# SSM tables and outputs in DRAM laid out for one transfer each, in a hybrid decoder layer on one core

## The chip, the core and the metric

The kernel runs on one core of a Trainium2 chip. The metric is the device time of one execution in microseconds (us); where several runs were made, their median. A profiled execution has its own time, and a span from its first to its last instruction that is a little shorter.

The engines are named as in the profile: PE multiplies matrices (PEld loads its weights), DVE works on vectors, ACT evaluates functions and copies, POOL is the general engine, SP issues transfers. Each engine runs its own list of instructions in order. An instruction that issues a DMA stands in such a list too, and those behind it wait for it.

## What is computed

One layer of a hybrid decoder over 1024 positions and 2048 channels, in float32:

```
h = rms_norm(x, norm_w);  proj = h @ w_in
q, k, v, a_gate, u, z, g_a, g_s = split(proj)
y_a = (window_attention(q, k, v, sinks) * silu(a_gate)) @ w_attn_proj
y_ssm = gelu(s5_ssm(u.reshape(b, l, 64 groups, 16)))          # 64 complex states in each group
glu_a, glu_b = split(y_ssm @ w_glu + b_glu)
y_s = (glu_a * sigmoid(glu_b) * silu(z)) @ w_ssm_proj
x = x + (sigmoid(g_a) * y_a + sigmoid(g_s) * y_s) @ w_out
```

`s5_ssm` runs, for each of the 64 groups, the diagonal recurrence s[t] = a s[t-1] + B u[t] with complex a (from A, log_dt), and gives y = Re(C s) + D u.

## The kernel before

**Projections.** Everything large is a product of 128 x 128 weight tiles with 512 positions. A float32 product is made of three: the weight and the activation are each split in a high and a low part (`split`, L80 to L82: ACT writes the high part by a cast, DVE the low part by a subtraction), and PE adds high x high, high x low and low x high (L121, L122, L125). `load_w` loads 512 KB of weights (8 tiles) by one DMA on SP (L106) into `wraw`, and the two casts make `whi` and `wlo`; each of the three has two buffers. Eight tiles are 24 matmuls of 512 columns.

**The stages** follow one another in the program: `uproj` (the SSM's input u) and the z gate with the preparation of the SSM tables beside them; `kvq` and attention; then the sigmoids and gates of the remaining columns with the SSM itself beside them; then the four products after it (`glu`, `att_out`, `ssm_out`, `out1` to `out3`), which split 2 x 2 blocks into seven products (Strassen), so that sums and differences of operand blocks have to be made first (`combos`).

**What sets the order.** The side work is written as generators that the main loop advances at given rates (`spawn`, `pull`, `drive`). Each engine's list is then fixed at build time by a scheduler that simulates the execution. An estimate of a shorter wait moves an instruction forward in its engine's list, and the engine then asks for its inputs earlier.

**The SSM in four batches of 16 groups.** `ssm_prep` computes powers of a (`wr`, `wi`; `p1`, `p2`; `al`, `be`), stores them in DRAM (PWD, PTD), and computes the table of the convolution within eight positions (`ks`), stored as KD behind 128 zeros. `ssm` does for each batch, in two halves q of eight groups:

- it loads the powers 16 times per half, eight times for the real and eight for the imaginary part, each to 16 partitions (`pwr`, `pwi`, L687), and B (`bre`, `bim`, L690);
- POOL makes `bm` from them in six operations (L665 by way of `tt`), PE multiplies it with u (`px`, L703), ACT copies the result to X;
- DVE and ACT run the recurrence on X;
- it loads `tz`, the shifted table, from KD by eight transfers (L744), POOL makes `ct`, PE makes `py` (L752, L753), ACT applies GELU to `yt`, and 16 transfers of 32 KB on SP store it in YD (L760).

`bm` and `tz` share one buffer, and `pwr`, `pwi`, `bre`, `bim`, `yt` have one each.

**What reads YD.** `combos` (L816) loads four 128 x 512 blocks (`cb_b`) for each of four k, DVE and POOL make four sums, and POOL stores them; it has five `cb` buffers. `load_ops` (L788) then loads operands (`op`) and splits them (`q1h`, `q6h`, ...: `q` and the number of the product).

**Constants for attention** (`c_qw`, `c_sk`, `c_blk`, `c_sel` and others) are loaded on POOL's queue after the last instructions of `ssm_prep`.

Of the kernel before, what the change touches and what calls it, by code (L numbers as in the profile page):

```python
# [9 lines left out]
F32 = mybir.dt.float32  # L10
# [14 lines left out]
NG = 64  # L25
# [7 lines left out]
def _build(nc, tc, I, OUT, ctx):  # L33
# [8 lines left out]
    dp = ctx.enter_context(tc.tile_pool(name="d", bufs=1, space=DRAM))  # L42
# [10 lines left out]
    CBD = {n: dp.tile([4, k, 128, TH], F32, name="cb" + n) for n, k in (("y", 4), ("a", 4), ("s", 4), ("m", 8))}  # L53
    QD = [dp.tile([8, 128, TH], F32, name=f"qd{n}") for n in range(3)]
    UD = dp.tile([8, 8, 128, NCH], F32, name="ud")
    YD = dp.tile([2, NG * 16, 8, 64], F32, name="yd")
    PWD = dp.tile([2, 8, NG, 64], F32, name="pwd")
    PTD = dp.tile([4, 128, 12, NG], F32, name="ptd")
    KD = dp.tile([16, NG, 256], F32, name="kd")

# [68 lines left out]
    def win(n):  # L129
        return [I["w_in"][n, :, c * KC:(c + 1) * KC, :] for c in range(2)]  # L130
# [89 lines left out]
    w = {(0, 0): load_w(win(12)[0], 2)}  # L220
    for kt in range(KT):
        if kt == 2:
            w[1, 0] = load_w(win(13)[0], 2)
        elif kt == 6 or kt == 8:
            n = kt // 8
# [228 lines left out]
    def ssm_prep(bp, pp):  # L454
        def tl(shape, tag, bufs=1, dt=F32, name=None):
            return bp.tile(list(shape), dt, tag=tag, bufs=bufs, name=name or tag)

        def tt(o, a, b, op, eng=None):
            (eng or V).tensor_tensor(o, a, b, op=op)
# [138 lines left out]
        cib = ci[0:64, 64:128].unsqueeze(1).to_broadcast([64, 8, 64])  # L598
        cmul(wr, wi, pr[0:64, 0:8, 64:128], pi[0:64, 0:8, 64:128], crb, cib, u2)
        for n, w in ((0, wr), (1, wi)):  # L600
            nc.gpsimd.dma_start(PWD[n].rearrange("j g p -> g j p"), w)

        p1, p2 = tl((128, 9, NG), "p1"), tl((128, 9, NG), "p2")
        V.tensor_copy(p1[0:64], pr[0:64, :, 0:64])
# [14 lines left out]
        for n in (9, 10, 11):  # L619
            p = slice(n - 1, n)  # L620
# [21 lines left out]
        for bt in range(4):  # L642
            ks = tl((16, GB, 8, 16), "ks")
            for q in range(GB // 8):
                g0 = bt * GB + q * 8
                ct = ctable(bp, tt, V, p1, p2, g0, 8, g0, 2)
                for qq in range(2):
                    pk = pp.tile([128, 4, 128], F32, tag="pa", bufs=2, name="pk")
                    for g in range(4):
                        gg = qq * 4 + g  # L650
                        PE.matmul(pk[0:16, g, :], bb[:, g0 + gg, :],
                                  ct[:, gg, 0:8, :].rearrange("p k h -> p (k h)"), start=True, stop=True)
                    S.copy(ks[:, q * 8 + qq * 4:q * 8 + qq * 4 + 4, :, :].rearrange("p g k h -> p g (k h)"),
                           pk[0:16])
                yield
            tt(ks[:, :, 0, :], ks[:, :, 0, :], dd[:, bt * GB:(bt + 1) * GB, :], add)
            nc.gpsimd.dma_start(KD[:, bt * GB:(bt + 1) * GB, 128:256],
                                ks.rearrange("p g k h -> p g (k h)"))

    def ssm(bp, pp):  # L660
        def tl(shape, tag, bufs=1, dt=F32, name=None):
            return bp.tile(list(shape), dt, tag=tag, bufs=bufs, name=name or tag)
# [6 lines left out]
        for bt in range(4):  # L669
            gs = bt * GB  # L670
# [11 lines left out]
            for q in range(2):  # L682
                g0 = gs + q * 8
                w = [tl((128, 8, 64), n, 1) for n in ("pwr", "pwi", "bre", "bim")]
                for n in range(2):
                    for j in range(8):
                        nc.sync.dma_start(w[n][16 * j:16 * j + 16],  # L687
                                          PWD[n, 7 - j, g0:g0 + 8, :].unsqueeze(0).to_broadcast([16, 8, 64]))
                for n, nm in ((2, "sBrT"), (3, "sBiT")):
                    nc.sync.dma_start(w[n], I[nm][:, g0:g0 + 8, :])  # L690
                bm = tl((128, 8, 2, 64), "bm", 1)
                u = tl((128, 8, 64), "bmu", 1)
                tt(bm[:, :, 0, :], w[0], w[2], mul, G)
                tt(u, w[1], w[3], mul, G)
                tt(bm[:, :, 0, :], bm[:, :, 0, :], u, sub, G)
                tt(bm[:, :, 1, :], w[0], w[3], mul, G)
                tt(u, w[1], w[2], mul, G)
                tt(bm[:, :, 1, :], bm[:, :, 1, :], u, add, G)
                for qq in range(2):
                    px = pp.tile([128, 4, 128], F32, tag="pa", bufs=2, name="px")  # L700
                    for g in range(4):
                        gg = qq * 4 + g
                        PE.matmul(px[:, g, :], bm[:, gg, :, :].rearrange("p a b -> p (a b)"),  # L703
                                  uq[:, q * 8 + gg, :], start=True, stop=True)
                    S.copy(X[:, q * 8 + qq * 4:q * 8 + qq * 4 + 4, :, 1:9, :].rearrange("p g h k s -> p g h (k s)"),
                           px.rearrange("p g (h c) -> p g h c", h=2))
                yield
# [32 lines left out]

            for q in range(2):
                tz = tl((128, 8, 128), "bm", 1, name="tz")
                for j in range(8):
                    nc.sync.dma_start(tz[16 * j:16 * j + 16],  # L744
                                      KD[:, gs + q * 8:gs + q * 8 + 8, 128 - 16 * j:256 - 16 * j])
                ct = ctable(bp, tt, G, p1, p2, gs + q * 8, 8, q * 8, 1)
                yt = tl((128, 8, NCH), "yt", 1)
                for qq in range(2):
                    py = pp.tile([128, 4, 128], F32, tag="pb", bufs=2, name="py")
                    for g in range(4):  # L750
                        gg = q * 8 + qq * 4 + g
                        PE.matmul(py[:, g, :], tz[:, qq * 4 + g, :], uq[:, gg, :], start=True, stop=False)  # L752
                        PE.matmul(py[:, g, :].rearrange("p (h c) -> p h c", h=2),  # L753
                                  ct[:, qq * 4 + g, 1:9, :].rearrange("p k h -> p (k h)"),
                                  X[:, gg, :, 0:8, :].rearrange("p h k s -> p h (k s)"), start=False, stop=True)
                    S.activation(yt[:, qq * 4:qq * 4 + 4, :], py, AF.Gelu_apprx_tanh)
                g0 = gs + q * 8
                for i in range(8):
                    for s in range(2):
                        nc.sync.dma_start(YD[s, g0 * 16:(g0 + 8) * 16, i, :].rearrange("(g h) c -> h g c", h=16),  # L760
                                          yt[16 * i:16 * i + 16, :, 64 * s:64 * s + 64])
                yield


# [10 lines left out]
    def unit(q, nk):  # L775
        p, t = (gp, "g") if q in IN_G[nk] else (hp, "h")
        return tuple(p.tile([128, TH], F32R, tag=t + x, name=f"q{q}{x}") for x in "hl")

    def load_ops(ops, src, nk, order, ks=None):

        todo = [(q, k) for q in order for k in ks or range(nk)]
        got = []

        def more(n):
            while todo and len(got) < n:
                q, k = todo.pop(0)
                t = staging()
                nc.sync.dma_start(t, src(q, k))  # L788
                got.append((q, t))

        more(STG - 1)
        yield
        while got:
            for _ in range(min(2, len(got))):
                q, t = got.pop(0)
                a, b = unit(q, nk)
                split(t, a, b)
                ops.setdefault(q, []).append((a, b))
                more(STG - 1)
            yield  # L800
# [10 lines left out]
    def combos(B, dst, nk):  # L811
        ct = lambda n: cbp.tile([128, TH], F32, tag="cb", bufs=5, name="cb_" + n)
        for k in range(nk):
            b = [ct("b") for _ in range(4)]
            for n, t in enumerate(b):
                nc.sync.dma_start(t, B(n // 2, n % 2, k))  # L816
            b11, b12, b21, b22 = b
            d7 = ct("d7")
            V.tensor_tensor(d7, b12, b22, op=SUB)
            G.tensor_tensor(b12, b11, b12, op=SUB)  # L820
            G.tensor_tensor(b22, b12, b22, op=ADD)
            V.tensor_tensor(b21, b21, b22, op=SUB)
            for n, t in enumerate((b12, b22, d7, b21)):
                nc.gpsimd.dma_start(dst[n, k], t)
            yield
# [364 lines left out]
    cbp = ctx.enter_context(tc.tile_pool(name="cb", bufs=1))  # L1190
    gp = ctx.enter_context(tc.tile_pool(name="g", bufs=12))
    p3 = ctx.enter_context(tc.tile_pool(name="p3", bufs=5, space=PSUM))
    By = lambda i, h, k: YD[h, (4 * i + k) * 128:(4 * i + k + 1) * 128].rearrange("p i c -> p (i c)")
    Ba = lambda i, h, k: AGD[h][4 * i + k]
    Bs = lambda i, h, k: SD[h][4 * i + k]
    Bm = lambda i, h, k: MD[h][8 * i + k]
# [36 lines left out]
def _layout(inputs):  # L1233
    A = {k: np.asarray(v) for k, v in inputs.items()}
# [7 lines left out]
    uc = ar(1024).reshape(8, 8, 16).transpose(0, 2, 1).reshape(-1)  # L1242
# [3 lines left out]
    def tiles(w):  # L1246
        k, n = w.shape
        return cc(w.reshape(k // 128, 128, n // 128, 128).transpose(2, 1, 0, 3))

    o = {}  # L1250
    o["xT"] = cc(A["x"][0].T).reshape(KT, 128, T)
    o["w_in"] = tiles(A["w_in"][:, cols])
    o["w_attn"] = tiles(A["w_attn_proj"][hc])
    o["w_glu"] = tiles(A["w_glu"])
    o["w_ssm"] = tiles(A["w_ssm_proj"])
    o["w_out"] = tiles(A["w_out"])
    o["nw"] = cc(A["norm_w"].reshape(KT, 128).T)
# [6 lines left out]
    i = ar(128)  # L1264
# [42 lines left out]
```

## Time and profile before

| | |
|---|---|
| three runs | 2544.15, 2546.79, 2549.72 us (median 2546.79) |
| profiled execution | 2542.53 us; its span 2540.8 us |
| busy share of the span | PE 97%, PEld 79%, DVE 61%, ACT 38%, POOL 36% |
| mean granted clock of PE | 0.988 of full speed |
| transfers | 438.95 MB, mean 173 GB/s |
| preparation of the tables | to about 205 us |
| SSM beside the projections | about 862 to 1360 us |
| combos and operands from YD | about 1360 to 1430 us, and 1732 to 1742 us |

Times within the execution count from the start of the span. A busy PE says little by itself, because matmuls overlap and their ends are modelled; the number of matmuls in a stretch tells whether it ran at its pace. A name in a row such as `px<-uq,bm` is what is written and what it is made from; `x16` is the count; `[3.38 <-POOL bm L665]` is idle time just before and what ended it.

### The profile page before, as it was taken

The numbers are of one execution on the slowest core, as the hardware profiler recorded it, in microseconds if no ns is written. First come the engines' busy times: TensorE is split into PE (matmuls) and PEld (weight loads), VectorE is DVE, ScalarE is ACT, GpSimd is POOL, SyncE is SP. The second block draws the span as 40 slices with busy tenths as digits, with TensorE's granted clock in tenths as the row PEclk, the third lists the DMA queues.
The fourth block names the chain that finished last, engine by engine and source line by source line (L and its number), as shares of the span: only waits on it lengthen the run. The fifth ranks groups of instructions, "written<-read, shape, count | busy, mean of one in ns | idle before, by whom it ended". The sixth has DMA issues, their size and how long they took to land. (4 is left out here: it accounts for less than half of the span.)

```text
span 2540.8 us, 30817 instructions
## 1 busy us (share of the span) xinstructions
PE 2459.2 (97%) x11012; PEld 2007.1 (79%) x11012; DVE 1557.5 (61%) x2040; ACT 963.8 (38%) x1492; POOL 921.5 (36%) x715
## 2 busy tenths in 40 slices
PE   7999999999999999999999999999999999899998
PEld 5878878788878878888788788887878877678886
DVE  7995566894686455736573432236587687745543
ACT  5333454463666433434442222224352331333311
POOL 5101004341453434251412300014547466414576
PEclk9999999999999999999999999999999999999999
DMA  6544343323223456565757743336368676888675
GB/s 212 177 135 133 92 141 104 96 72 99 96 92 121 141 161 165 177 166 142 206 159 240 259 164 124 120 120 216 108 223 296 203 252 227 266 298 278 222 234 176
DMA packets 217306, 438.95 MB, mean 173 GB/s; under 512 B 63521, under 2 KB 75841, under 8 KB 217153
## 3 DMA queue, kind: packets, MB, share of 16 engines
q1 hardware_dynamic: 181376, 344.34, 44.4%
q0 software_dynamic: 19504, 63.28, 6.6%
q10 hardware_dynamic: 16272, 29.38, 3.0%
q8 instruction: 86, 1.41, 0.2%
q14 instruction: 68, 0.55, 0.1%
HBM read 341.93 MB, written 94.96 MB: 172 GB/s over the span
## 5 line engine op out<-in xcount | busy, mean ns | idle before, releaser
L121 PE MATMUL ps<-hh,whi 128*128 128x512 f32 x2144 | 845.3, 395 | 4.7 <-ACT whi L81 4.7
L122 PE MATMUL ps<-hl,whi 128*128 128x512 f32 x2144 | 842.1, 393 | 1.0 <-DVE hl L144 1.0
L82 DVE TENSOR_TENSOR wlo<-wraw,whi 128x1024 fp32r<-128x1024 f32 (+1 forms) x344 | 445.2, 1295 | 488.9 <-PE ps L125 247.7
L81 ACT CAST whi<-wraw 128x1024 fp32r<-128x1024 f32 (+1 forms) x344 | 349.8, 1018 | 637.2 <-PE ps L122 372.0
L125 PE MATMUL ps<-hh,wlo 128*128 128x512 f32 x2144 | 542.0, 391 | 1.7 <-DVE wlo L82 1.7
L121 PEld LDWEIGHTS ps<-hh,whi 128*128 128x128 f32 x2144 | 405.1, 189 | 93.8 <-ACT whi L81 6.4
L122 PEld LDWEIGHTS ps<-hl,whi 128*128 128x128 f32 x2144 | 405.3, 189 | 86.7 <-DVE hl L144 2.1
L125 PEld LDWEIGHTS ps<-hh,wlo 128*128 128x128 f32 x2144 | 401.5, 188 | 86.9 <-DVE wlo L82 2.1
L81 ACT CAST whi<-ws 128x1024 fp32r<-128x1024 f32 x80 | 84.2, 1054 | 292.5 <-POOL ws L855 80.4
L82 DVE TENSOR_TENSOR wlo<-ws,whi 128x1024 fp32r<-128x1024 f32 x80 | 116.4, 1456 | 115.7 <-ACT whi L81 74.4
L855 POOL TENSOR_TENSOR ws<-wraw 128x512 f32<-128x512 f32 (+1 forms) x72 | 135.0, 1875 | 132.9 <-DVE wlo L82 95.8
L421 POOL TENSOR_TENSOR pa<-ph,c_mct 128x512 fp32r<-128x512 f32 x32 | 43.7, 1364 | 253.3 <-ACT ph L81 253.2
L178 POOL DMA_DIRECT2D gsd<-sg x32 | 17.8, 556 | 226.7 <-ACT sg L177 214.8
L177 ACT ACTIVATE sg<-sg 128x512 f32<-128x512 f32 x64 | 40.6, 634 | 136.5 <-DVE sg L176 136.4
L402 ACT ACTIVATE scs<-scs,m,rq 128x128 f32<-128x128 f32 x128 | 62.2, 487 | 61.9 <-DVE m L396 61.8
L1000 POOL TENSOR_TENSOR mt<-mt,pa 128x512 f32<-128x512 f32 x32 | 56.3, 1762 | 74.9 <-DMA sgs<-gsd 22.6
L178 POOL DMA_DIRECT2D gd<-sg x32 | 17.7, 555 | 177.7 <-ACT sg L177 165.3
L861 PE MATMUL psm<-q1h,whi 128*128 128x512 f32 x160 | 64.7, 405 | 6.8 <-ACT whi L81 6.8
L861 PE MATMUL psm<-q4h,whi 128*128 128x512 f32 x160 | 66.2, 414 | 3.0 <-DVE mt L995 3.0
L862 PE MATMUL psm<-q4l,whi 128*128 128x512 f32 x160 | 65.6, 410 | 1.4 <-DVE q4l L82 1.4
L861 PE MATMUL psm<-q2h,whi 128*128 128x512 f32 x160 | 62.7, 393 | 2.7 <-ACT qa L892 2.6
L862 PE MATMUL psn<-q3l,whi 128*128 128x512 f32 x160 | 62.8, 393 | 1.6 <-DVE q3l L82 1.6
(352 smaller groups left out, 4165.7 us busy)
## 6 DMA issues: line engine op xcount, KB each, us to landing
wraw<-w_in SPq DMA_DIRECT2D x268, 512.0 KB, 3.6
wraw<-w_out SPq DMA_DIRECT2D x72, 512.0 KB, 5.2
x<-xT SPq DMA_DIRECT2D x96, 256.0 KB, 3.9
gd<-sg POOLq DMA_DIRECT2D x32, 256.0 KB, 3.7
gsd<-sg POOLq DMA_DIRECT2D x32, 256.0 KB, 2.9
wraw<-w_glu SPq DMA_DIRECT2D x16, 512.0 KB, 4.2
wraw<-w_attn SPq DMA_DIRECT2D x16, 512.0 KB, 4.7
sga<-gd SPq DMA_DIRECT2D x32, 256.0 KB, 4.4
```

The source lines that it names most:

```text
L81: S.copy(hi, src)
L82: V.tensor_tensor(lo, src if src2 is None else src2, hi.bitcast(F32), op=ALU.subtract)
L121: PE.matmul(ps, hi[:, kk, :], rh[kt], start=(kt == 0), stop=False)
L122: PE.matmul(ps, hi[:, kk, :], rl[kt], start=False, stop=False)
L125: PE.matmul(ps, lo[:, kk, :], rh[kt], start=False, stop=(kt == last))
L177: S.activation(sg, sg, AF.Sigmoid)
L402: S.activation(sc[:, r, :], sc[:, r, :], AF.Exp, bias=m4[:, r:r + 1], scale=RQ[h, p][:, b, 2 * r + e:2 * r + e + 1], accum_out=den[:, r:r ...
L421: G.tensor_tensor(a, ph.bitcast(F32), mb, op=ALU.mult)
L855: G.tensor_tensor(o, a, b, op=ADD)
L861: PE.matmul(ps, hi[:, c0 + k, :], rh, start=(first and k == 0), stop=False, skip_group_check=True)
L862: PE.matmul(ps, hi[:, c0 + k, :], rl, start=False, stop=False, skip_group_check=True)
L1000: G.tensor_tensor(t, t, p, op=ADD)
```

## The change

Four layouts in DRAM change, and with them the transfers:

- **PWD** holds every power 16 times, in the order of the 128 partitions. `ssm_prep` writes it by 16 transfers on POOL's queue (256 KB each, in pieces of 256 bytes) where there were two (128 KB each). `ssm` reads `pwr` and `pwi` by one transfer each per half (16 in all, where there were 128).
- **TZD** is new: the shifted table for all groups. `ssm_prep` copies it from KD, DRAM to DRAM, by eight transfers of 512 KB on POOL's queue behind the last store to KD. `ssm` reads `tz` by one transfer per half (8, where there were 64).
- **YD** is stored as `yt` lies: two transfers of 256 KB per half (16, where there were 128), issued by ACT instead of SP. Its readers, `cb_b` (16 transfers) and `op<-yd` (12), now gather 1024 pieces of 256 bytes each where they read 128 rows of 2 KB.
- **w_glu**'s rows are permuted on the host to the new order of the channels; its transfers are as before.

The list of SP has 930 instructions where it had 1226, that of ACT 14 more, that of POOL 22 more. PE's has the same number of matmuls in another order.

```
-    YD = dp.tile([2, NG * 16, 8, 64], F32, name="yd")
-    PWD = dp.tile([2, 8, NG, 64], F32, name="pwd")
+    YD = dp.tile([2, 8, 128, 8, 64], F32, name="yd")
+    PWD = dp.tile([2, 8, 16, NG, 64], F32, name="pwd")
+    TZD = dp.tile([128, NG, 128], F32, name="tzd")
...
-            nc.gpsimd.dma_start(PWD[n].rearrange("j g p -> g j p"), w)
+            for j in range(8):
+                nc.gpsimd.dma_start(PWD[n, 7 - j].rearrange("h g p -> g h p"),
+                                    w[:, j, :].unsqueeze(1).to_broadcast([64, 16, 64]))
...
+        for j in range(8):
+            nc.gpsimd.dma_start(TZD[16 * j:16 * j + 16], KD[:, :, 128 - 16 * j:256 - 16 * j])
...
-                    for j in range(8):
-                        nc.sync.dma_start(w[n][16 * j:16 * j + 16],
-                                          PWD[n, 7 - j, g0:g0 + 8, :].unsqueeze(0).to_broadcast([16, 8, 64]))
+                    nc.sync.dma_start(w[n], PWD[n, :, :, g0:g0 + 8, :].rearrange("j h g p -> (j h) g p"))
...
-                for j in range(8):
-                    nc.sync.dma_start(tz[16 * j:16 * j + 16],
-                                      KD[:, gs + q * 8:gs + q * 8 + 8, 128 - 16 * j:256 - 16 * j])
+                nc.sync.dma_start(tz, TZD[:, gs + q * 8:gs + q * 8 + 8, :])
...
-                g0 = gs + q * 8
-                for i in range(8):
-                    for s in range(2):
-                        nc.sync.dma_start(YD[s, g0 * 16:(g0 + 8) * 16, i, :].rearrange("(g h) c -> h g c", h=16),
-                                          yt[16 * i:16 * i + 16, :, 64 * s:64 * s + 64])
+                for s in range(2):
+                    nc.scalar.dma_start(YD[s, 2 * bt + q], yt[:, :, 64 * s:64 * s + 64])
...
+    def like(t, src):
+        return t if len(src.shape) == 2 else t.rearrange("p (i c) -> p i c", i=src.shape[1])
...
-                nc.sync.dma_start(t, src(q, k))
+                nc.sync.dma_start(like(t, src(q, k)), src(q, k))
...
-                nc.sync.dma_start(t, B(n // 2, n % 2, k))
+                nc.sync.dma_start(like(t, B(n // 2, n % 2, k)), B(n // 2, n % 2, k))
...
-    By = lambda i, h, k: YD[h, (4 * i + k) * 128:(4 * i + k + 1) * 128].rearrange("p i c -> p (i c)")
+    By = lambda i, h, k: YD[h, 4 * i + k].rearrange("(i h) g c -> (h g) i c", h=16)
...
-    o["w_glu"] = tiles(A["w_glu"])
+    o["w_glu"] = tiles(A["w_glu"][uc])
```

The list of SP at the start of the first SSM batch, before:

```order
L673 DMA be<-ptd 128x12x16
L676 DMA uq<-ud 128x1024 x2
L687 DMA pwr<-pwd 16x512 x4
L106 DMA wraw<-w_in 128x1024
L687 DMA pwr<-pwd 16x512 x4
L687 DMA pwi<-pwd 16x512 x6
L106 DMA wraw<-w_in 128x1024
L687 DMA pwi<-pwd 16x512 x2
L690 DMA bre<-sBrT 128x512
L690 DMA bim<-sBiT 128x512
```

and the same place with the change:

```order
L678 DMA be<-ptd 128x12x16
L681 DMA uq<-ud 128x1024 x2
L691 DMA pwr<-pwd 128x512
L691 DMA pwi<-pwd 128x512
L693 DMA bre<-sBrT 128x512
L693 DMA bim<-sBiT 128x512
L107 DMA wraw<-w_in 128x1024
```

The 16 loads of the powers are two, and both loads of B have moved ahead of the two weight loads (`wraw`) that stood between.

The list of SP through the last two rounds of `combos` on YD, up to the first operands (`op<-yd`), before:

```order
L816 DMA cb_b<-yd 128x512 x3
L106 DMA wraw<-w_in 128x1024
L788 DMA op<-cby 128x512
L816 DMA cb_b<-yd 128x512
L106 DMA wraw<-w_in 128x1024
L816 DMA cb_b<-yd 128x512 x3
L106 DMA wraw<-w_in 128x1024
L788 DMA op<-yd 128x512
```

and with the change:

```order
L817 DMA cb_b<-yd 128x8x64
L789 DMA op<-cby 128x512
L107 DMA wraw<-w_in 128x1024
L817 DMA cb_b<-yd 128x8x64
L107 DMA wraw<-w_in 128x1024
L817 DMA cb_b<-yd 128x8x64 x2
L107 DMA wraw<-w_in 128x1024
L817 DMA cb_b<-yd 128x8x64
L107 DMA wraw<-w_in 128x1024
L789 DMA op<-yd 128x8x64
```

Between the last block of one round and the last block of the next stand two weight loads before and three with the change. Counted over all four rounds, the weight loads between these are 3, 2 and 2 before, and 4, 4 and 3 with the change, whose first round begins four weight loads earlier.

The list of POOL at the end of the preparation, where the constants of attention are loaded, before:

```order
L628 DMA ptd<-be 128x768
L193 DMA zd_76<-sg 128x512
L657 DMA kd<-ks 16x16x128
L64 DMA c_mct<-mct 128x128
L64 DMA c_mpt<-mpt 128x128
L1152 DMA maskq<-maskq 128x128
L64 DMA c_qw<-qw 128x1
```

and with the change:

```order
L631 DMA ptd<-be 128x768
L194 DMA zd_76<-sg 128x512
L660 DMA kd<-ks 16x16x128
L663 DMA tzd<-kd 1024x128 x8
L65 DMA c_mct<-mct 128x128
L65 DMA c_mpt<-mpt 128x128
L1153 DMA maskq<-maskq 128x128
L65 DMA c_qw<-qw 128x1
```

The eight copies to TZD stand between the last store to KD and the constants; the load of `c_blk` follows three rows later (four before).

On PE, the first `px` stands behind 3232 matmuls of the projections where it stood behind 3245. In the four batches 49, 49, 53 and 49 of them stand between the `px` of the first half and that of the second, where there were 49, 55, 62 and 43.

## Rows read from the trace of the kernel before

**Rows 1.** The page's part 1: busy us (share of the span) xinstructions of each engine.

```profile
PE 2459.2 (97%) x11012; PEld 2007.1 (79%) x11012; DVE 1557.5 (61%) x2040; ACT 963.8 (38%) x1492; POOL 921.5 (36%) x715
```

**Rows 2.** Busy time by stretch, PE: stretch, us, PE busy (xmatmuls), PEclk, DMA, GB/s.

```profile
1500.00:1550.00 50.00, 50.00 (x222) 1.00 0.38 121
...
890.00:910.00 20.00, 16.61 (x74) 0.91 0.63 179
...
1020.00:1040.00 20.00, 18.04 (x88) 1.00 0.74 208
1250.00:1270.00 20.00, 16.40 (x69) 0.91 0.71 217
1405.00:1430.00 25.00, 18.83 (x70) 0.86 0.78 265
```

**Rows 3.** Timeline of PE: start us, us, line, matmul, [idle before <-releaser].

```profile
902.43 3.06 PE L703 MATMUL px<-uq,bm 128*128 128x128 f32 x16 [3.38 <-POOL bm L665]
...
1030.54 2.05 PE L703 MATMUL px<-uq,bm 128*128 128x128 f32 x16 [1.96 <-POOL bm L665]
...
1257.88 3.48 PE L703 MATMUL px<-uq,bm 128*128 128x128 f32 x16 [2.61 <-POOL bm L665]
...
1420.42 0.80 PE L121 MATMUL ps<-hh,whi 128*128 128x512 f32 x1 [4.20 <-ACT whi L81]
```

**Rows 4.** Timeline of SP: start us, us, line, transfers issued.

```profile
866.83 1.45 SPq L676 DMA_DIRECT2D uq<-ud  x2
...
1242.79 0.43 SPq L687 DMA_DIRECT2D pwi<-pwd  x1
```

**Rows 5.** Timeline of POOL in the first half and in the last.

```profile
883.27 2.06 POOL L665 TENSOR_TENSOR bm<-pwr,bre 128x512 f32<-128x512 f32 x1 [9.13 <-DMA c<-sC]
...
901.13 1.25 POOL L665 TENSOR_TENSOR bm<-bm,bmu 128x512 f32<-128x512 f32 x1
...
1232.91 1.28 POOL L665 TENSOR_TENSOR bmu<-pwi,bre 128x512 f32<-128x512 f32 x1
...
1247.52 1.32 POOL L665 TENSOR_TENSOR bm<-pwr,bre 128x512 f32<-128x512 f32 x1 [4.95 <-DMA bre<-sBrT]
...
1255.70 2.13 POOL L665 TENSOR_TENSOR bm<-bm,bmu 128x512 f32<-128x512 f32 x1
```

**Rows 6.** DMA issues: names, queue, xcount, KB each, median us from issue to landing.

```profile
ud<-ut POOLq DMA_DIRECT2D x16, 256.0 KB, 3.4
...
op<-yd SPq DMA_DIRECT2D x12, 256.0 KB, 3.9
...
bre<-sBrT SPq DMA_DIRECT2D x8, 256.0 KB, 4.1
...
p<-ptd SPq DMA_DIRECT2D x8, 72.0 KB, 4.4
```

**Rows 7.** Timeline of SP: the last blocks of three rounds of combos.

```profile
1376.19 1.62 SPq L816 DMA_DIRECT2D cb_b<-yd  x3
...
1390.03 3.69 SPq L816 DMA_DIRECT2D cb_b<-yd  x3
...
1404.65 2.83 SPq L816 DMA_DIRECT2D cb_b<-yd  x3
```

**Rows 8.** Timeline of ACT: the first operand's cast, ahead of a weight's.

```profile
1418.80 0.62 ACT L81 CAST q1h<-op 128x512 fp32r<-128x512 f32 x1 [11.84 <-DMA op<-yd]
```

**Rows 9.** Timeline of PE at the third product of the gated unit.

```profile
1737.10 0.50 PE L861 MATMUL psn<-q3h,whi 128*128 128x512 f32 x1 [1.00 <-ACT q3h L81]
```

**Rows 10.** One line on POOL: duration ns min/median/max, first and last start us.

```profile
L206 POOL DMA_DIRECT2D ud<-ut x16: 885/914/985, 62.3 to 471.1; - x16
```

**Rows 11.** Timelines of POOL, DVE and PE at the constants of attention.

```profile
206.03 0.54 POOL L64 DMA_DIRECT2D c_mct<-mct  x1 [4.39 <-DMA kd<-ks]
...
217.69 0.22 DVE L74 CAST c_blk<-cr_blk 128x128 fp32r<-128x128 f32 x1
...
232.84 0.40 PE L300 MATMUL pk<-sqh,c_blk 128*128 128x512 f32 x1
```

## The prediction

> **What bounds the kernel now.** I read the busy shares first [rows 1]: PE is at 97%, so a transfer or another engine can only matter where PE waits. Because a busy PE is not yet PE at its pace, I then went through the busy times in stretches of 50 us. In undisturbed stretches PE does 222 matmuls of 512 columns in 50 us, 0.225 us each, at the full granted clock (the first of [rows 2]). So eight weight tiles, 24 matmuls, last 5.4 us, and that is how often a load of weights is used up.
>
> Between 855 and 1430 us, where the change works, four stretches fall short [rows 2]. The timeline of PE names the waits in them [rows 3]: three times `px` waits for `bm` from POOL, once a projection waits for the high part of its weight. In three of the four the granted clock's mean over the stretch is 0.86 to 0.91, so part of it ran at the lower level, 1.2 GHz, right after the idle time. Counting matmuls takes in both. A `px` block of 16 small matmuls lasts 2.05 us at full clock (1030.54 in [rows 3]); the rest at 0.225 each:
>
> - 890 to 910: 58 x 0.225 + 2.05 = 15.1 of 20 us, short by 4.9.
> - 1020 to 1040: 72 x 0.225 + 2.05 = 18.3 of 20, short by 1.7.
> - 1250 to 1270: 53 x 0.225 + 2.05 = 14.0 of 20, short by 6.0.
> - 1405 to 1430: 70 x 0.225 = 15.8 of 25, short by 9.2.
>
> Together 21.8 us, 0.86% of the run: the most that the change can give back here.
>
> **The change part by part.** *First half of the first batch.* SP has issued u by 868.28 and then needs 16 issues for the powers, with weight loads between [rows 4]; POOL starts `bm` at 883.27 and ends at 902.38, 19.1 us later [rows 5]. Now four issues follow u, 0.43 us each: 870.0. B lands 4.1 us after its issue [rows 6], so POOL starts at 874.1, and with one store of 0.5 us more between its operations it ends at 874.1 + 19.6 = 893.7. PE began to wait at 902.43 - 3.38 = 899.05; it now comes 13 matmuls, 2.9 us, earlier: 896.1. Margin 2.4 us, and the 4.9 us go.
>
> *Second halves.* In the last batch POOL is done with the first half's `pwi` at 1234.2 but the last load of the new one goes out at 1242.79 [rows 4], behind the rest of 16 stores and 16 loads on SP; `bm` starts at 1247.52 after 4.95 us of waiting for B and ends at 1257.83, 10.3 us later [rows 5]. Now SP issues `pwi` and `bre` at 1234.2 to 1235.1; with 4.1 us to land POOL could go on at 1239.2, right behind its first half. It needs 10.3 and a store of 0.6: 10.9. PE leaves it 49 matmuls and a `px` block: 11.0 + 2.05 = 13.1. Margin about 1.7 us, in the second batch too; 1.7 and 6.0 go.
>
> *The end of the SSM and `combos`.* The wait at 1420.42 is for a weight whose load had come in time: ACT stood 11.84 us at the cast of the first operand from YD, ahead of the weight's [rows 8]. That operand was late because the rounds of `combos` end on SP at 1377.8, 1393.7 and 1407.5 [rows 7], 13.8 to 15.9 us apart, while the order puts only two weight loads, 10.9 us of PE's work, between rounds: SP holds up the weights at each. The change's order has four and three: 21.7 and 16.3 us, at or above 15.9. The operand's cast still stands before the same weight's, but PE is no longer behind. The 9.2 us go.
>
> These margins, 0.4 to 2.4 us, are thin: one and the same `bm` product took 1.32 and 2.06 us [rows 5]. I take a quarter off: 0.75 x 21.8 = 16.4 us. I keep all of it, and up to 1 us more from a fourth, shorter wait, for the range.
>
> *YD read in pieces of 256 bytes.* 28 loads. The nearest rows: a write of 256 KB in such pieces lands in 3.4 us, the present read in rows of 2 KB in 3.9, a read of 72 KB in 1152 pieces of 64 bytes in 4.4 [rows 6]. So from -0.5 to, if small pieces cost a full DMA more, +4 us. Most lie beside PE's work; four do not: the third product waits for its operands as they land [rows 9]. I take +1.5, range 0 to +4.
> By the Trainium skill (DMA: Bandwidth & Descriptors, section Specifications) a transfer needs pieces of 512 bytes for full rate and is worse below. The write row does not show that; by the page alone the upper end would be nearer.
>
> *Stores to YD from ACT.* 16 issues, at 0.43 us as on SP about 7 us over 500; ACT is idle 62% of the span [rows 1], and each follows the GELU that it waits for anyway, so nothing queues behind a foreign wait. A weight's cast is at most 0.9 us later, and behind two buffers each of raw and of split weights that is nothing. If a cast were already late, it would cost these 0.9 us, twice per batch.
>
> *`tz` by one transfer.* Its second load follows `py` of the first half on SP; PE now comes back after 30 matmuls, 6.8 us, where it was 83. Issue 0.4, landing about 4.1 to 4.4: 1.9 us to spare. Taken as nothing; four times 1 us for the range.
>
> *Preparation.* 16 stores of powers where there were 2: a DMA of 1024 pieces costs POOL 0.91 us [rows 10], so two blocks of 7.3 us, each ahead of one store of the z gate. Its buffer is asked for 20 instructions later in DVE's new list, so the delay is hidden; without that cover DVE, and behind it the gate's PSUM bank, would wait up to 7.3 us. The eight copies to TZD stand ahead of the constants: they begin when KD has landed, where the constants began before, at 206.03 [rows 11], or up to 4 us later, since one z store more now stands ahead of KD's last. With 8 x 0.91 = 7.3 us of issue the constants begin by 217, 11 us later than before, and `c_blk`, ready at 217.9 before, by 229. PE asked at 232.84 [rows 11], now 8 matmuls later, 234.6. I take +1, range 0 to +4; more is a rival.
>
> **Sum:** -16.4 + 1.5 + 1 = -13.9 us. The profiled execution's 2542.53 becomes 2528.6; the median of the runs shown lies 4.3 higher, so 2532.9, rounded to 2533. 0.2% is 5.1 us, about what a measurement of this kernel can tell from no change: faster means under 2541.7, slower over 2551.9.
>
> **The rivals.**
> *The waits move with the order.* The scheduler lets PE ask earlier wherever it believes a transfer shorter, so the `px` waits return at about their old size, and only `combos` gives: -0.75 x 9.2 + 2.5 = -4.4, 2542. For: the waits of before came from the same scheduler. Against: the margins above, and an unchanged distance from the last `py` to the next `px`.
> *Hidden anyway.* `bm` is held by what is left (the C table is named as its releaser at 883.27 in [rows 5]), `combos` by landings and buffers; nothing is gained, the 2.5 us are paid: 2549. Against: in SP's list the named loads stand behind the 16.
> The Trainium skill has this as a rule (DMA: Bandwidth & Descriptors, section Issuing engines are not separate DMA queues): issuing elsewhere saves only the issue time, small beside the transfer. Here [rows 4] show that the 16 issues of 0.43 us, 6.9 us, come one after another in one chain.
> *Slower: the constants behind TZD.* The eight copies and the constants share POOL's queue. If the data of the copies hold the constants back until after 234.6, PE stands at `pk`, each further us costs one. 256 KB land in 3.4 us [rows 6]; copies of 512 KB one after another would take 8 x 6.8 = 54 us, to 264, 30 us too late. From 19 us too late (254) it eats the 13.9 and 5 more. Half way between, 24 us: 2533 - 1 + 24 = 2556. Against: transfers overlap, and 7.3 us of issue is the nearer row.
>
> **How the numbers follow.** Forecast 62% (own range 2521 to 2541), moved waits 17% (2538 to 2546), hidden 12% (2546 to 2552), slower 9%. Low end: all 21.8 and 1 more, less 2.5 of cost, and the runs' spread: 2521. High end: over the moved waits and half of the hidden case: 2549. That leaves out some 18%. Faster: 60 of the forecast's 62 and 8 of the 17: 68%. Within 0.2%: 2 + 9 + 12 = 23%. Slower 9%.
>
> **What would show it.** Right: no idle of PE at `px` over 1 us; 222 matmuls per 50 us around the end of the SSM; `bm` of the first half started 9 us after the loads of the powers began or sooner; rounds of `combos` 16 to 22 us apart without a late weight. Costs: idle at the third product near 2 us; `c_blk` cast by 230 us. Wrong: new waits of PE for `tz` or `ct` at the second `py` (a gain under 8 us), a long wait at `pk`, or landings of `cb_b` well over 5 us with rounds over 16.3 us apart, which would bring the weight's wait back.

## Result and the profile after

The changed kernel takes 2523.28 us (median of 4 runs, 2522.15 to 2524.47) against 2548.26 (2544.15 to 2554.0) for the kernel before on the same chip: a ratio of 0.990, 95% interval 0.988 to 0.992. The forecast was 2533, with a range of 2521 to 2549: the kernel is faster, as said, and by 10 us more than that. The two profiled executions lie 19 us apart (2542.53 and 2523.69), the medians 25; where the other 6 us are was the first thing that the experiments had to find.

The page's part 1 of after answers to [rows 1]; PE is busy 6.2 us less for the same 11012 matmuls:

```profile
PE 2453.0 (97%) x11012; PEld 2004.9 (80%) x11012; DVE 1564.3 (62%) x2040; ACT 958.5 (38%) x1490; POOL 928.9 (37%) x737
```

Busy time by stretch of after, PE (columns as in [rows 2]). The stretches lie around the same work as the four short ones there: the first `px`, the second half of the second batch, that of the last, and the end of `combos`:

```profile
886.00:906.00 20.00, 18.57 (x91) 1.00 0.58 178
1002.00:1022.00 20.00, 20.00 (x98) 1.00 0.63 200
1228.00:1248.00 20.00, 20.00 (x100) 1.00 0.47 149
1385.00:1410.00 25.00, 25.00 (x112) 1.00 0.94 272
```

Where before had 74, 88, 69 and 70 matmuls, there are 91, 98, 100 and 112. The granted clock is full in all four, and only the first has idle time left. Next come the waits of PE between 850 and 1440 us (line, what it waited for: us in total, times, longest): first the three longest of before, in its second profiled execution (`before_again` below), then all of after:

```profile
PE px L703 <- POOL bm L665: 14.1, 5, 5.0
PE ps L121 <- ACT whi L81: 4.3, 1, 4.3
PE ps L125 <- DVE wlo L82: 2.2, 1, 2.2
```

```profile
PE px L706 <- POOL bm L670: 1.4, 1, 1.4
PE ps L122 <- ACT hh L144: 1.2, 1, 1.2
PE ps L123 <- DVE hl L145: 0.5, 2, 0.3
```

SP's timeline of after at the first half of the first batch answers to [rows 4], POOL's to [rows 5], PE's to [rows 3]:

```profile
868.95 1.35 SPq L681 DMA_DIRECT2D uq<-ud  x2
870.35 0.43 SPq L691 DMA_DIRECT2D pwr<-pwd  x1
870.82 0.43 SPq L691 DMA_DIRECT2D pwi<-pwd  x1
871.29 0.49 SPq L693 DMA_DIRECT2D bre<-sBrT  x1
871.83 0.44 SPq L693 DMA_DIRECT2D bim<-sBiT  x1
```

```profile
878.01 1.28 POOL L670 TENSOR_TENSOR bm<-pwr,bre 128x512 f32<-128x512 f32 x1 [13.49 <-DMA bre<-sBrT]
...
897.49 1.26 POOL L670 TENSOR_TENSOR bm<-bm,bmu 128x512 f32<-128x512 f32 x1
...
1226.20 1.28 POOL L670 TENSOR_TENSOR bm<-pwr,bre 128x512 f32<-128x512 f32 x1 [0.46 <-PE px L706]
...
1232.30 1.30 POOL L670 TENSOR_TENSOR bm<-bm,bmu 128x512 f32<-128x512 f32 x1
```

```profile
898.80 2.05 PE L706 MATMUL px<-uq,bm 128*128 128x128 f32 x16 [1.43 <-POOL bm L670]
...
1012.70 1.95 PE L706 MATMUL px<-uq,bm 128*128 128x128 f32 x16
...
1237.08 1.95 PE L706 MATMUL px<-uq,bm 128*128 128x128 f32 x16
```

Four issues follow u as expected. `bm` begins 3.9 us later than I worked out and ends 5.1 us later (898.75), so 1.4 us of the first wait stay. In the last batch `bm` does not wait for a load any more (0.46 us for `px`), and is done 3.5 us before PE asks.

### The profile page after: what moved, and what is told of

It is laid out like the page before. It is cut to its first block, busy times and chain, and to the rows that moved or that the text cites. A ratio compares the mean times of both kernels' runs of the same rounds, so it can differ in the third digit from the quotient of the medians.

```text
span 2521.8 us, 30481 instructions
## 1 busy us (share of the span) xinstructions
PE 2453.0 (97%) x11012; PEld 2004.9 (80%) x11012; DVE 1564.3 (62%) x2040; ACT 958.5 (38%) x1490; POOL 928.9 (37%) x737
## 5 line engine op out<-in xcount | busy, mean ns | idle before, releaser
L83 DVE TENSOR_TENSOR wlo<-wraw,whi 128x1024 fp32r<-128x1024 f32 (+1 forms) x344 | 458.1, 1333 | 515.5 <-PE ps L126 291.4
L83 DVE TENSOR_TENSOR wlo<-ws,whi 128x1024 fp32r<-128x1024 f32 x80 | 121.8, 1523 | 111.8 <-ACT whi L82 74.0
L179 POOL DMA_DIRECT2D gsd<-sg x32 | 17.7, 553 | 248.1 <-ACT sg L178 225.2
L179 POOL DMA_DIRECT2D gd<-sg x32 | 17.8, 555 | 182.1 <-ACT sg L178 173.7
```

The lines of the kernel that those rows point to most:

```text
L83: V.tensor_tensor(lo, src if src2 is None else src2, hi.bitcast(F32), op=ALU.subtract)
```

## Experiments

All were timed in five rounds beside the kernel before on the same chip, whose median was 2551.4, 2550.8 and 2549.9 in the three groups of four. Two tables gather what they gave. The first shows where time goes along the run. Its median is that of the kernel's own runs; its other columns are of one execution. They give the start, in us, of the n-th matmul of a projection or product (those that write `ps`, `psm` or `psn`, 9888 of the 11012), less that of the second execution of before, whose own starts are in the first row. A step between two columns is time won or lost between them: at the first half's `px`, at the other `px`, at `combos`, and behind.

| kernel | median us | 2737th | 3337th | 4753rd | 5401st | last |
|---|---|---|---|---|---|---|
| before, second execution | 2549.7 | 764.5 | 931.2 | 1299.8 | 1463.4 | 2535.8 |
| before, first execution | 2548.3 | -0.7 | -1.4 | -6.8 | -7.3 | -7.4 |
| p_only | 2532.6 | 0.4 | -6.8 | -15.2 | -17.8 | -16.8 |
| t_only | 2548.7 | -0.5 | -1.4 | -7.6 | -5.1 | -2.5 |
| y_only | 2537.7 | 0.6 | -0.6 | -5.7 | -15.6 | -11.9 |
| no_t | 2528.8 | -0.6 | -7.7 | -16.7 | -26.6 | -19.2 |
| before_pieces | 2538.8 | 1.5 | 0.7 | -2.3 | -12.2 | -9.5 |
| p_pieces | 2527.6 | 0.3 | -7.0 | -17.7 | -27.7 | -22.2 |
| y_rows | 2537.0 | -1.0 | -8.4 | -20.1 | -18.5 | -15.9 |
| after, first | 2523.3 | 0.6 | -5.1 | -16.5 | -26.5 | -26.0 |
| after, second | 2526.2 | 0.2 | -6.7 | -16.3 | -26.2 | -23.8 |
| y_sync | 2524.4 | -1.0 | -8.3 | -20.0 | -29.9 | -25.9 |
| combos_pool | 2541.7 | 0.4 | -0.2 | -4.0 | -8.0 | 1.6 |
| tzd16 | 2528.0 | 6.6 | -0.1 | -11.9 | -21.8 | -19.8 |

The second table is on the rounds of `combos`. It gives the weight loads (without the two of `w_glu`) that SP's order puts between the last load of one round and that of the next, and beside them PE's matmuls from 1390 to 1450 us (266 is full pace):

| kernel | weight loads between rounds | matmuls |
|---|---|---|
| before (first, second) | 3, 2, 2 | 225, 222 |
| t_only | 3, 2, 3 | 225 |
| p_only | 3, 3, 2 | 234 |
| y_rows | 4, 2, 2 | 233 |
| y_only | 3, 4, 3 | 266 |
| p_pieces | 4, 3, 4 | 267 |
| before_pieces | 4, 4, 3 | 266 |
| no_t | 3, 4, 3 | 267 |
| after | 4, 4, 3 | 266 |

**before_again**: the kernel before, no edit.

> The kernel before, unchanged, to see a second execution of it in the profile: its runs spread over 11 us (2544 to 2555 us), while those of the changed kernel spread over 2 to 5, and the execution profiled at first was the fastest of them. Theory (the waits that the change removes are what spreads): a run near the median of 2551 shows the same waits, longer, at px of the second halves and at the weight's end of the SSM, 14 to 18 us short there in all more than the changed kernel has. Rival (the spread comes from elsewhere, the gated unit or the preparation): the same 9.3 us at px and 4.5 at the weight between 850 and 1440 us, and the rest in stretches that the change doesn't touch.

2549.66 us (2545.48 to 2553.83, 11 runs); the profiled execution took 2550.86. `px` waited 14.1 us in it (row above), against 9.3 in the first; by the 4753rd matmul it is 6.8 us behind the first, 5.4 of them after the 3337th. So what the change removes is larger in a usual execution than in the one that I had read, and varies. The base of the forecast was a short one. Behind the 5401st the distance moves between 4.3 and 10.5 us, which I can't assign.

**p_only, t_only, y_only, after_again**: one part each, and the whole again.

```
p_only: PWD = dp.tile([2, 8, 16, NG, 64], ...), its 16 stores,
        nc.sync.dma_start(w[n], PWD[n, :, :, g0:g0 + 8, :]...)
t_only: TZD, its 8 copies, nc.sync.dma_start(tz, TZD[:, gs + q * 8:...])
y_only: YD[s, 2 * bt + q] stored from ACT, By in pieces, w_glu[uc]
```

> Only the powers change (PWD written 16 times over, one load for pwr and one for pwi per half); TZD and YD as before. Theory (each wait belongs to the part that shortened its loads): the three px waits go or shrink as in the changed kernel, 4 + 2 + 3 us, since SP still has 16 stores to YD and 8 loads of tz between; the weight's wait at the end of the SSM stays, because it belongs to YD: -8 us, 2540 against 2548. Rival 1 (the wait at the end goes with the number of weight loads that the order puts between rounds of combos, whatever makes the order; here 3, 3 and 2 where before had 3, 2, 2): part of its 9 us goes too, -13. Rival 2 (the powers were hidden behind the stores to YD on SP): within 2 us of before.

> Only TZD (eight copies in the preparation, one load for tz per half); powers and YD as before. Theory: nothing is won, PE never waited for tz; 0 to -2 us, and the wait for the constants at pk, late by at most 1 us, may show. Rival 1 (SP's issues count wherever they stand: 7 fewer per half, 3 us, before loads that are waited for): -4 to -6. Rival 2 (constants behind TZD): +1 to +4.

> Only YD (stored as it lies, from ACT, read in 256-byte pieces, rows of w_glu ordered to fit); powers and tables as before. Theory: the weight's wait at the end of the SSM goes (9 us), the first px wait stays at 3 to 5 us, the px waits of the second halves shrink by the 16 stores that SP no longer has, 2 to 4 us together: -12. Rival (the second halves' waits come from the 16 loads of powers alone and the end's wait from the landings of YD's operands, which get longer): -5 or less, with idle time at the cast of the first operand from YD of 8 us or more.

> The changed kernel once more, beside the three parts on one chip. If the parts add up, it stands at the sum of the three, -19 to -21 us. If one fewer stop of SP hides another (each part alone frees the same waits), it is less than the sum; if a wait only goes when all its loads are short, it is more than the sum. Its distance from the kernel before also tells whether the difference of 25 us in the medians or of 19 us in the two profiles is the one that repeats.

Measured: 2532.64 (ratio 0.993, 0.992 to 0.994), 2548.71 (0.999, 0.998 to 1.000), 2537.68 (0.994, 0.993 to 0.996), 2526.22 (0.990, 0.989 to 0.991). The powers give 18.8 us, over twice what I wrote: in p_only no `px` waits, though SP still has its 16 stores. In place of those waits, PE waits once for `py` in the last batch, and the weight's wait stays (PE's waits of p_only, 850 to 1340, then 1340 to 1440):

```profile
PE py L752 <- issue: 3.2, 1, 3.2
PE ps L122 <- DVE hl L144: 0.7, 1, 0.7
```

```profile
PE ps L121 <- ACT whi L81: 4.0, 1, 4.0
```

At that `py` (1255.47) SP has just issued the eight loads of `tz`, the last at 1250.93:

```profile
1244.30 4.70 SPq L744 DMA_DIRECT2D tz<-kd  x6
...
1250.93 0.30 SPq L744 DMA_DIRECT2D tz<-kd  x1
```

That last load landed at 1255.28, 0.2 us before `py` began. So once the powers come early, PE comes to `py` early, and `tz` is next. y_only frees the end (266 matmuls) and shortens the `px` waits to 5.9 us, as expected. The three parts sum to -35.3 us, the whole is -25.2. By the first table 6.3 us of y_only's gain lie at `px`, where p_only removes the waits anyway, and 2.6 of p_only's at `combos`: taken once, some 26 are left. This is argued and not shown, because the two executions of before differ by 6.1 us in the same columns. The whole repeats at -25, so the difference of the medians is the one that repeats.

**no_t, y_sync**: the change without TZD; and with the stores to YD from SP.

```
-                    nc.scalar.dma_start(YD[s, 2 * bt + q], yt[...])
+                    nc.sync.dma_start(YD[s, 2 * bt + q], yt[...])
```

> The changed kernel without TZD: powers and YD changed, tz loaded by 8 loads per half from KD as before. Theory: TZD is worth nothing once the other two are in, PE never waits for tz, and the constants of attention come up to 11 us earlier without the eight copies ahead of them: within 2 us of the changed kernel's 2526, so 2524 to 2527. Rival 1 (the 14 issues that SP is spared before the second half's loads count): 2528 to 2531. Rival 2 (the copies hold the constants back and cost the changed kernel 1 to 4 us): 2522 to 2524.

> The changed kernel with the two stores per half to YD issued from SP instead of ACT, where they wait for the GELU with weight loads behind them. Theory: what counted was 16 issues against 2, not the queue: 0 to +2 us against the changed kernel. Rival (a store at the head of SP's queue holds back weights until the GELU is done, and PE waits for a weight in each half): +4 us or more.

no_t took 2528.77 (2522.65 to 2532.51, 6 runs), which overlaps the changed kernel's two series and lies 2.6 and 5.5 above their medians; its profile is level with the changed kernel's up to the 5401st matmul. What its execution lacks, it loses behind the 6721st (still -26.7 there), where nothing reads `tz`. Its `py` did not wait either: in the last batch the eight loads of `tz` had landed 2.7 us before it. So the trace shows no worth of TZD here, and the medians leave 0 to 5 us open. y_sync took 2524.36 (2523.02 to 2526.34): with two stores per half the queue made no difference.

**y_rows**: the change with YD read in rows of 2 KB.

```
-    By = lambda i, h, k: YD[h, 4 * i + k].rearrange("(i h) g c -> (h g) i c", h=16)
+    By = lambda i, h, k: YD[h, 4 * i + k]
```

> The changed kernel with YD read in whole rows of 2 KB per partition instead of eight pieces of 256 bytes; the channels then come in another order, so that the gated unit multiplies rows of the weights with the wrong channels. Nothing else changes. Theory as predicted: the small pieces cost 1.5 us in all, so -1.5 (2524 to 2525). Rival 1 (hidden everywhere): within 0.7 us of the changed kernel. Rival 2 (each first operand lands later by a full DMA): -4.

2536.98 (2533.19 to 2543.92): 11 to 14 us slower, against all three expectations. The first table shows the place: it is level with the best up to the 4753rd matmul, and then lacks the 10 us that after gains by the 5401st. With whole rows the scheduler puts the rounds close together again (4, 2, 2), and PE waits for weights as it did before (PE's timeline of y_rows):

```profile
1387.23 0.50 PE L122 MATMUL ps<-hh,whi 128*128 128x512 f32 x1 [2.71 <-ACT whi L82]
...
1432.34 0.79 PE L122 MATMUL ps<-hh,whi 128*128 128x512 f32 x1 [2.59 <-ACT whi L82]
```

That led to a sharper theory: the 10 us at `combos` come from the order, and the order from the shape of the read.

**before_pieces, p_pieces, combos_pool**: before with YD's token block ahead of the channel, so that it is read in pieces of 256 bytes; the same with the powers' part; before with the rounds' loads on POOL's queue.

```
-    YD = dp.tile([2, NG * 16, 8, 64], F32, name="yd")
+    YD = dp.tile([2, 8, NG * 16, 64], F32, name="yd")
-    By = ... YD[h, (4*i+k)*128:(4*i+k+1)*128].rearrange("p i c -> p (i c)")
+    By = ... YD[h, :, (4*i+k)*128:(4*i+k+1)*128].rearrange("i p c -> p i c")

combos_pool:
-                nc.sync.dma_start(t, B(n // 2, n % 2, k))
+                nc.gpsimd.dma_start(t, B(n // 2, n % 2, k))
```

> The kernel before with one thing changed: YD has the token block ahead of the channel in DRAM, so that combos and the first operands read it in eight pieces of 256 bytes instead of rows of 2 KB. The 16 stores to YD stay on SP, in pieces of 256 bytes as before; powers and tables stay. The order is that of before up to the rounds of combos, and has 4, 4 and 3 weight loads between the rounds where before had 3, 2 and 2. Theory (the weight's wait at the end of the SSM hangs on how many weight loads stand between the rounds, and small reads matter only through that): the 10 us of that wait go, the px waits stay: -10, 2541 against 2551. Rival 1 (the wait goes because YD is stored early, in few stores and from ACT): nothing goes, 2551. Rival 2 (small reads cost what they cost by their size): +2 to +4.

> The powers' part of the change plus the reading of YD in pieces of 256 bytes as in before_pieces; YD still by 16 stores from SP, no TZD, rows of w_glu as before. The order has 4, 3 and 4 weight loads between the rounds of combos. Theory (all of the gain is px waits, which go with the powers, and the weight's wait, which goes with the order of the rounds): as fast as the changed kernel, 2523 to 2527. Rival (the few stores from ACT and TZD carry gain of their own): 2529 or more, 4 us over the changed kernel.

> The kernel before with the loads of the combos rounds issued from POOL's queue instead of SP's, so that no weight load stands behind them; nothing else changes. Theory (SP stops at each round until a buffer is free, with weight loads behind): the weight's wait at the end of the SSM goes, -8 to -10: 2542. Rival 1 (ACT stands at the cast of the first operand from YD, whatever queue loads it, and the weight's cast behind it): 2551, with idle time of 10 us at that cast. Rival 2 (POOL, which adds and subtracts in the rounds, now stops for buffers, so that rounds take longer and operands come later): +3 or more.

before_pieces: 2538.76 (0.995, 0.994 to 0.997), -11.1, with all 16 stores still on SP. Busy time by stretch, PE, of before, of before_pieces and of combos_pool:

```profile
1390.00:1450.00 60.00, 53.83 (x225) 0.94 0.80 273
```

```profile
1390.00:1450.00 60.00, 60.00 (x266) 1.00 0.88 266
```

```profile
1390.00:1450.00 60.00, 56.38 (x241) 0.97 0.78 254
```

So few stores and ACT's queue are not needed to remove that wait. The order is not separated from the shape, because no run has one without the other; but the pieces by themselves did not make the rounds' loads faster (5.5 us from issue to landing, against 4.6 in rows), so what gains is most likely the order. p_pieces took 2527.55 (2526.66 to 2532.36): two edits to the layout give all but 1 to 4 us of the change. Its profile has one wait of 2.2 us for `py` left, as p_only has; no_t, which also loads `tz` eight times but stores YD by two transfers from ACT, has none, so TZD is not the only thing that removes it.

combos_pool, 2541.73 (0.997, 0.996 to 0.998), gains 8 us. Its profiled execution, the second slowest of its twelve runs, has 4.0 of them at `combos`, and PE still runs short at the end, by 25 matmuls or 5.6 us. Weights no longer stand behind the rounds on SP; the rounds end at 1384.7, 1400.7 and 1418.6 on POOL, 16 and 18 us apart, while SP issues two and then four weight loads, and ACT still stands at the operand's cast ahead of a weight's (ACT's timeline of combos_pool; [rows 8] had 11.84, after has 4.48):

```profile
1429.59 0.62 ACT L81 CAST q1h<-op 128x512 fp32r<-128x512 f32 x1 [7.79 <-DMA op<-yd]
```

```profile
1397.36 0.62 ACT L82 CAST q1h<-op 128x512 fp32r<-128x512 f32 x1 [4.48 <-DMA op<-yd]
```

So SP's stops are a part of it. That ACT's order is the other part, and that more of PE's work between rounds helps with both, fits these rows but was not tested by itself. A round takes 16 to 19 us on POOL, and 13 to 20 on SP over these runs.

**tzd16**: the copies to TZD issued twice.

```
+            for _ in range(2):
                 nc.gpsimd.dma_start(TZD[16 * j:16 * j + 16], KD[...])
```

> The changed kernel with each of the eight copies to TZD issued twice, so 16 copies of 512 KB stand ahead of the constants of attention on POOL's queue. It tests the rival by which the copies hold up the constants. Theory (a further copy is only issued when an earlier one has landed, about 2 us each, so that c_blk comes some 15 us later, at 249 us, where PE asks for it at 234.6): a wait of 12 to 16 us at pk, 2537 to 2541. Rival (only the issues count, 0.75 us each): c_blk 6 us later, 2530 or less.

2528.01 (2525.75 to 2530.96), 2 to 5 us over the changed kernel. It tested less than it should: the scheduler put the last eight copies among and behind the constants, not ahead. Casts of `c_blk` on DVE and `pk` on PE, after, then tzd16:

```profile
233.93 0.22 DVE L75 CAST c_blk<-cr_blk 128x128 fp32r<-128x128 f32 x1
234.60 0.40 PE L301 MATMUL pk<-sqh,c_blk 128*128 128x512 f32 x1
```

```profile
238.01 0.23 DVE L75 CAST c_blk<-cr_blk 128x128 fp32r<-128x128 f32 x1 [0.90 <-DMA cr_blk<-blk]
238.34 0.47 PE L301 MATMUL pk<-sqh,c_blk 128*128 128x512 f32 x1 [0.39 <-issue]
```

`c_blk` comes 4.1 us later and `pk` 3.7, and by the 2737th matmul PE is 6.0 to 6.4 us behind the two executions of after: the changed kernel has no time to spare there.

## Why the prediction held, and where its sizes were off

*First half.* Right in sum: between the 2737th and the 3337th matmul after gains 5.0 us on the first execution of before, and 6.2 in its own second one, where 4.9 and up to 1 from a shorter wait had been worked out. The margin of 2.4 us was wrong: it came out at -1.4 in one execution and just enough in the other. SP reached u 2.1 us later (868.95 against 866.83 in [rows 4]), and `bm` began 6.7 us after the issue of B at 871.29, not 4.1 [rows 6]. The error in the margin, 3.8 us, was larger than the margin; that only 1.4 us of the wait came of it, and none in the other execution, is in part luck.

*Second halves.* Right in place, 6.0 us (3337th to 4753rd, after -11.4, before -5.4) where 7.7 were worked out; against the second execution of before it is 11.4. The margin was 3.5 us, not 1.7: POOL had done the first of the six products earlier, and the rest took 7.4 us, not 10.9.

*End of the SSM and `combos`.* The 9.2 us went (9.5 by the table, 10.0 on the second execution), by the weights between rounds, as worked out. What I had not asked is which part of the change makes that order: the small reads, not the stores. The rounds of after end on SP at 1352.0, 1369.0 and 1386.6:

```profile
1349.34 2.62 SPq L817 DMA_DIRECT2D cb_b<-yd  x2
...
1368.63 0.39 SPq L817 DMA_DIRECT2D cb_b<-yd  x1
...
1385.92 0.69 SPq L817 DMA_DIRECT2D cb_b<-yd  x1
```

17.0 and 17.6 us apart, longer than before's [rows 7], with 21.7 and 16.3 us of PE's weights between: the mark of 16.3 was passed by 1.3 us without a late weight. By the prediction's own sign, landings of `cb_b` over 5 us (here 5.6) with rounds over 16.3 us apart would have brought the wait back; they did not.

*The quarter off* was the term most at fault. Between the 2737th and the 5401st matmul after gains 20.5 us on the first execution of before (27.1 less 6.6), 94% of the ceiling of 21.8, not 75%.

*Small reads, +1.5.* No cost is seen in PE's time. The loads of the operands land as before ([rows 6]: 3.9); those of the rounds took 5.6, where they took 4.6 before and 4.7 in y_rows (DMA issues of after, columns as in [rows 6]):

```profile
cb_b<-yd SPq DMA_DIRECT2D x16, 256.0 KB, 5.6
op<-yd SPq DMA_DIRECT2D x12, 256.0 KB, 3.9
```

The third product waited 1.76 us where it was 1.00 [rows 9], but from the 5401st to the 6721st matmul after and before gain alike on the second execution of before (2.7 and 2.5 us). The sign was wrong: through the order these pieces are worth 11 us.
The Trainium skill (DMA: Bandwidth & Descriptors, section Specifications) has pieces under 512 bytes lose rate. Here the rounds' loads bear that out a little (on SP 5.5 to 6.2 us to landing in pieces over the runs, 4.6 to 4.9 in rows), those of the operands hardly (3.9 to 4.7, against 3.2 to 3.9).

*Preparation, +1.* `c_blk` was ready at 234.15 instead of 229; by the 2737th matmul after stands 0.9 to 1.3 us behind the first execution, 0.2 to 0.6 behind the second. The size is about right, but by luck: only the issues of the copies to TZD (7.3 us) were counted, and their data held the constants back (last section).

*The rivals.* Moved waits and hidden waits fell: no `px` waits in p_only. The slower rival's mechanism was there, and stopped within a microsecond of costing time: `c_blk` was ready 0.45 us before `pk` began at 234.60.
By the Trainium skill (DMA: Bandwidth & Descriptors, section Issuing engines are not separate DMA queues) an issue is usually small beside its transfer, so that another issuing engine saves little: y_sync agrees. One load of the powers fits too, 0.43 us to issue [rows 4] and 2.1 to land (median of the 64 of `pwr`, before), but 16 in a chain are 6.9 us. p_only, which makes two of them and with that moves other loads forward, gained 18.8.

*The base.* 4.3 us were added for the median of three runs. Usual executions of before lie 7 to 9 above the one profiled; in the second execution that distance is there by the 5401st matmul (7.3 us), most of it at `px`. The change removed it with those waits: after's median is its profile. So the miss of 9.6 us is 4.3 of base that did not carry over, 4.1 of the quarter (5.4 taken off, 1.3 lost), some 0.6 of costs (2.5 taken, 1.3 seen by the 2737th matmul and 0.6 behind the 5401st), and 0.6 that this account doesn't place.

## What to carry to other kernels

Where a scheduler orders loads by their described shape, the layout of a buffer in DRAM moves the order. Here that was worth 11 us, while each transfer itself took 1 us longer. So count what stands between two rounds in each engine's order, and set it beside the time that a round takes. Merging many small loads paid where their issues form a chain ahead of something that PE waits for, and the next chain then came to the front (`tz` in p_only). Before taking one profile as the base, see how far it lies from the other runs: a spread that a change removes is gain that the profile doesn't show.

## What was not expected of the hardware

Small loads that were issued behind large copies on POOL's queue landed behind them. The eight copies to TZD were issued from 208.93 on, 0.75 us each, and landed between 213.4 and 231.2. `c_mct` went out right behind them, without a wait, and landed only at 231.7, 16.8 us later; without the copies it took 2.1 us (no_t). All seven constants up to `cr_blk` landed between 231.7 and 233.4, and none of the 277 DMAs of this queue in the trace of after landed before one issued ahead of it (DMA issues, columns as in [rows 6], of after, then of no_t):

```profile
tzd<-kd POOLq DMA_DIRECT2D x8, 512.0 KB, 11.5
c_mct<-mct POOLq DMA_DIRECT2D x1, 64.0 KB, 16.8
```

```profile
c_mct<-mct POOLq DMA_DIRECT2D x1, 64.0 KB, 2.1
```

From the third constant on, the issues wait as well (timeline of POOL, after):

```profile
208.93 6.02 POOL L663 DMA_DIRECT2D tzd<-kd  x8 [2.61 <-DMA kd<-ks]
...
219.55 0.53 POOL L1153 DMA_DIRECT2D maskq<-maskq  x1 [3.42 <-DMA tzd<-kd]
221.69 0.54 POOL L65 DMA_DIRECT2D c_qw<-qw  x1 [1.61 <-DMA tzd<-kd]
225.00 0.53 POOL L65 DMA_DIRECT2D c_kw<-kw  x1 [2.77 <-DMA tzd<-kd]
```

These waits come from the program. Its DMAs on POOL's queue use eight semaphores in turn, and each of the five waits up to `cr_blk`, 11.3 us in all, ended 0.3 us after the landing of the DMA eight places ahead. They did little to hold `c_blk` back, since `c_mct`, which did not wait, landed only 1.7 us ahead of `cr_blk`. I had counted issues alone (7.3 us); the data of the copies, 22.3 us from the first issue to the last landing, are why `c_blk` came 5 us later than worked out.
